# Gate tile of the dense experts in two buffers, v in three, and gate columns from two rounded matmuls per token

## The chip, the cores and the metric

The kernel runs on one core of one Trainium2 chip. The metric is the device time of one execution in microseconds (us). The core has five engines that run beside each other, each through its own list of instructions in a fixed order: PE (TensorE, matmuls; PEld is its loading of weights), DVE (VectorE), ACT (ScalarE), POOL (GpSimd) and SP (SyncE, which here only issues DMA transfers). An instruction starts when its turn has come on its engine and the results and buffers that it needs are there.

## The reference

One layer of a hybrid encoder on 1024 tokens of width 1024: an attention branch and a convolution branch, gated and merged, and then a layer of 128 x 128 single-neuron experts (PEER), of which each token uses 16 for each of 8 heads. The change lies in this last layer.

```python
def peer_ffn(hn, w_query, sub_keys, expert_u, expert_v):
    ...
        q = (xc @ w_query).reshape(c, PEER_HEADS, 2, PEER_HALF_DIM)
        sc = jnp.einsum('chpd,hpnd->chpn', q, sub_keys).astype(jnp.float32)
        s1, i1 = lax.top_k(sc[:, :, 0], PEER_TOPK)
        s2, i2 = lax.top_k(sc[:, :, 1], PEER_TOPK)
        cand = (s1[..., :, None] + s2[..., None, :]).reshape(c, PEER_HEADS, PEER_TOPK * PEER_TOPK)
        cidx = (i1[..., :, None] * PEER_N_KEYS + i2[..., None, :]).reshape(c, PEER_HEADS, PEER_TOPK * PEER_TOPK)
        top, pos = lax.top_k(cand, PEER_TOPK)
        eidx = jnp.take_along_axis(cidx, pos, axis=-1)
        g = jax.nn.softmax(top, axis=-1)
        u = expert_u[eidx]
        a = jax.nn.gelu(jnp.einsum('chkd,cd->chk', u, xc), approximate=False)
        vv = expert_v[eidx]
        return jnp.einsum('chk,chkd->cd', (g.astype(a.dtype) * a), vv)
```

## The kernel before

**Precision.** The large matmuls keep float32 precision by splitting each operand into a high part in the rounded 32-bit format (F32R) and a low part, the rest, in the same format. ACT writes the high part, DVE subtracts it to get the low one, and three products (high by high, high by low, low by high) are added in PSUM.

**Two groups of tokens.** Group B is five tiles of 128 tokens (`NB`), group A is three (`NA`). B goes through projection, attention, convolution, output and scores first, then A does. The scores of A are the last matmuls ahead of the expert layer.

**The two ways through the expert layer.** Group B is computed densely: all 128 rows of 128 experts are multiplied by all 640 tokens, and a gate matrix `w_d` in DRAM, zero wherever a token did not choose an expert, picks what counts. Group A gathers: for each token, POOL issues indirect DMAs that fetch the rows u and v of the chosen experts (`fetch`, L739, 384 transfers of 1 MB into `UVT` = 4 buffers), DVE forms the dot product with the token (L746) and, after two small ACT instructions (L748, L749), adds v times the result to `acc` (L755). The gather and the dense loop share DVE and the DMA engines.

**Selection.** `select_gen` finds the 16 best of each head on DVE with one multiply on POOL in each of its pieces (L639). A tile of tokens is selected in two halves, each of four heads. The five tiles of B feed the gate matrix, the three tiles of A the gather.

**The gate matrix.** `weights_gen` works in 160 steps of four tokens (`WQ`), 32 for each tile of B. In a step DVE compares the chosen row and column numbers with a row of counters, which gives two one-hot blocks `ms` (L714). POOL multiplies the first by the gate weights to `o1` (L718, the tile is shown as o), ACT copies the second to `o2` (L720), PE forms one 128 x 128 product for each of the four tokens (`pw`, L695), ACT copies them to `wbuf` (L696), and every eighth step the buffer goes to `w_d` (L726). The trace shows two records for each such float32 product, 1280 in all. `weights_gen`, the selection and the gather are generators: the phases that run beside them call `tick`, which lets them emit a step after so many estimated microseconds. The framework's scheduler then orders the emitted instructions on each engine by its own estimate of times.

**The dense loop.** For expert row i, `expert_in` loads u (`raw`, L913), splits it, forms `z` by 48 matmuls of 320 columns (L905), applies Gelu (L929) and multiplies by the gate tile `wt` (L930), which is loaded for four rows at once (`WB`, 1.28 MB, L920). The product is split to `ph`, `phl`. `expert_v` loads and splits v (`vh`, `vhl`). `expert_out` handles a pair of rows (`BLK`): 60 matmuls of 512 columns; two of the five token tiles stay in PSUM (`held`), three go through two PSUM buffers (`pout`) and are added to `hacc` by DVE (L957). All loads of u, v and wt are issued by SP in one queue.

```python
            wts[b] = dn.tile([P, GB // WT, WB, WT], F32, name="wt", tag="wt", bufs=1)
            SP.dma_start(out=wts[b], in_=w_d[:, :, i:i + WB, :].rearrange("c p i t -> p c i t"))
```

## Time and profile before

| what | value |
|---|---|
| time, median of 3 runs | 3235.85 us (3223.81 to 3254.53) |
| time of the profiled execution | 3236.47 us |
| its span, first to last instruction | 3234.7 us |
| busy share of the span | PE 93%, DVE 82%, ACT 40%, POOL 30% |
| mean granted TensorE clock | 0.973 of full speed |
| first and last Gelu of the dense loop | 1323.0 and 3153.1 us |
| last addition to hacc | 3181.1 us |

Times in the rows are counted from the start of the span. The shares are averages over the whole program; the stages are the projection and attention of B (to about 724 us), attention, convolution and output of A with most of the gate matrix beside them (to 1204), the scores of A (to 1312), the dense loop with the gather beside it (to 3181), and what is left of the gather (to the end).

### The profile page before, as it was taken

The numbers are of one execution on the slowest core, as the hardware profiler recorded it, in microseconds if no ns is written. First come the engines' busy times: TensorE is split into PE (matmuls) and PEld (weight loads), VectorE is DVE, ScalarE is ACT, GpSimd is POOL, SyncE is SP. The second block draws the span as 40 slices with busy tenths as digits, with TensorE's granted clock in tenths as the row PEclk, the third lists the DMA queues.
The fourth block names the chain that finished last, engine by engine and source line by source line (L and its number), as shares of the span: only waits on it lengthen the run. The fifth ranks groups of instructions, "written<-read, shape, count | busy, mean of one in ns | idle before, by whom it ended". The sixth has DMA issues, their size and how long they took to land.

```text
span 3234.7 us, 46047 instructions
## 1 busy us (share of the span) xinstructions
PE 3017.4 (93%) x17551; PEld 2768.1 (86%) x17551; DVE 2647.0 (82%) x4665; ACT 1298.3 (40%) x2344; POOL 954.6 (30%) x716
## 2 busy tenths in 40 slices
PE   7999999898999889799999999999999999999992
PEld 6799988798888779798989989889888999998891
DVE  4442565478999996798999999999999999998898
ACT  3322464335567757433333333333333333333332
POOL 2310000045444444232223323322333323233333
PEclk9999999999999989899999999999999999999996
DMA  5451232555444374787888888878789899988997
GB/s 177 146 177 66 82 111 92 211 164 202 146 177 182 148 269 161 265 297 274 304 291 293 308 286 315 323 275 316 268 301 339 325 348 338 339 329 317 327 331 288
DMA packets 237550, 801.12 MB, mean 248 GB/s; under 512 B 18832, under 2 KB 123280, under 8 KB 174096
## 3 DMA queue, kind: packets, MB, share of 16 engines
q0 software_dynamic: 64704, 442.53, 37.4%
q1 hardware_dynamic: 152592, 305.30, 27.2%
q10 hardware_dynamic: 20032, 50.34, 4.1%
q8 instruction: 138, 2.26, 0.3%
q14 instruction: 84, 0.69, 0.1%
HBM read 714.74 MB, written 83.36 MB: 247 GB/s over the span
## 4 chain that ended last, share of the span: by engine, by line
PE 36%; DVE 20%; issue 18%; DMA 15%; POOL 7%; ACT 3%; SPq 0%; POOLq 0%; ACTq 0%; DVEq 0%
DMA wt<-w_d 7%; PE z L905 7%; POOL uvt L739 6%; PE pg L228 4%; DMA uvt<-in_uv,idx 4%; PE pq L228 4%; PE pout L905 4%; DVE acc L755 3%; PE ph L228 3%; DVE uvt L746 3%; PE held L905 2%; PE py L228 2%; PE pw L695 2%; DVE hacc L957 2%; PE pv L228 1%
## 5 line engine op out<-in xcount | busy, mean ns | idle before, releaser
L739 POOL DMA_INDIRECT uvt<-in_uv,idx x384 | 552.6, 1439 | 1297.0 <-DVE acc L755 852.8
L905 PE MATMUL z<-actTh,uh 128*128 128x320 f32 x2048 | 636.7, 311 | 2.1 <-ACT pr L929 1.1
L905 PE MATMUL z<-actTh,uhl 128*128 128x320 f32 x2048 | 637.6, 311 | 0.0
L905 PE MATMUL z<-actTl,uh 128*128 128x320 f32 x2048 | 636.1, 311 | 0.0
L746 DVE SCALAR_TENSOR_TENSOR uvt<-uvt,hng 128x1024 f32<-128x1024 f32 x384 | 472.7, 1231 | 48.6 <-DMA uvt<-in_uv,idx 42.9
L755 DVE SCALAR_TENSOR_TENSOR acc<-uvt,wt,acc 128x1024 f32<-128x1024 f32 x381 | 486.4, 1277 | 6.1 <-ACT wt L749 4.8
L905 PEld LDWEIGHTS z<-actTh,uh 128*128 128x128 f32 x2048 | 387.1, 189 | 12.2 <-ACT pr L929 2.1
L905 PEld LDWEIGHTS z<-actTl,uh 128*128 128x128 f32 x2048 | 387.4, 189 | 8.8
L905 PEld LDWEIGHTS z<-actTh,uhl 128*128 128x128 f32 x2048 | 387.9, 189 | 4.0
L905 PE MATMUL pout<-vh,ph 128*128 128x512 f32 x768 | 306.5, 399 | 47.0 <-DVE hacc L957 30.2
L748 ACT ACTIVATE wt<-zt 128x1 f32<-128x1 f32 x384 | 77.5, 202 | 668.4 <-DVE uvt L746 667.5
L905 PE MATMUL pout<-vhl,ph 128*128 128x512 f32 x768 | 302.7, 394 | 0.0
L905 PE MATMUL pout<-vh,phl 128*128 128x512 f32 x768 | 301.9, 393 | 0.6 <-DVE phl L898 0.6
L718 POOL TENSOR_TENSOR o<-ms,wtr 128x512 f32<-128x512 bf16 x160 | 204.7, 1322 | 256.5 <-PE pw L695 127.3
L957 DVE TENSOR_TENSOR hacc<-pout,hacc 128x512 f32<-128x512 f32 x384 | 260.5, 681 | 2.8 <-PE pout L905 2.8
L185 DVE TENSOR_TENSOR wl<-wr,wh 128x2048 fp32r<-128x2048 f32 x66 | 157.2, 2382 | 118.8 <-ACT wh L184 114.7
L896 ACT CAST ph<-pr 128x640 fp32r<-128x640 f32 x128 | 93.3, 729 | 394.2 <-DVE pr L930 394.2
L905 PEld LDWEIGHTS pout<-vh,ph 128*128 128x128 f32 x768 | 145.7, 190 | 78.7 <-DVE hacc L957 39.5
L695 PE MATMUL pw<-o,o 128*128 128x128 f32 x1280 | 172.3, 288 | 39.8 <-POOL o L718 20.2
L184 ACT CAST wh<-wr 128x2048 fp32r<-128x2048 f32 x74 | 141.1, 1909 | 168.8 <-DMA wr<-in_wq 41.5
L695 PEld LDWEIGHTS pw<-o,o 128*128 128x128 f32 x1280 | 164.3, 201 | 47.7 <-POOL o L718 26.9
L905 PE MATMUL held<-vh,ph 128*128 128x512 f32 x512 | 200.6, 392 | 0.7 <-ACT ph L896 0.7
(290 smaller groups left out, 6760.4 us busy)
## 6 DMA issues: line engine op xcount, KB each, us to landing
raw<-in_uT SPq DMA_DIRECT2D x128, 512.0 KB, 6.5
raw<-in_uv SPq DMA_DIRECT2D x128, 512.0 KB, 8.0
w_d<-wbuf ACTq DMA_DIRECT2D x20, 2048.0 KB, 7.0
wt<-w_d SPq DMA_DIRECT2D x32, 1280.0 KB, 16.0
wr<-in_wcols SPq DMA_DIRECT2D x28, 1024.0 KB, 5.1
wr<-in_wq SPq DMA_DIRECT2D x24, 1024.0 KB, 5.2
xt<-in_x SPq DMA_DIRECT2D x16, 512.0 KB, 4.0
q_d<-qt POOLq DMA_DIRECT2D x32, 256.0 KB, 3.5
```

Source lines behind the costliest of these rows:

```text
L184: A.copy(out=op[0][sl], in_=src)
L185: lo.tensor_sub(op[1][sl], src, op[0][sl].bitcast(F32))
L228: PE.matmul(pd, lhsT=l[a], rhs=r[b], start=i == 0 and j == 0, stop=i == n - 1 and j == len(c) - 1)
L695: PE.matmul(pw[:, u, :], lhsT=o2[:, t + u, :], rhs=o1[:, t + u, :], start=True, stop=True)
L718: PL.tensor_tensor(out=o1.rearrange("p t i -> p i t"), in0=ms[:, 0], in1=w[:, ts].unsqueeze(1).broadcast_to(sh), op=ALU.mult)
L739: PL.indirect_dma_start(out=t[:], out_offset=None, in_=uv, in_offset=bass.IndirectOffsetOnAxis(ap=sels[c][1][:, k:k + 1], axis=0))
L746: V.scalar_tensor_tensor(u, u, 1.0, st[c], op0=ALU.mult, op1=ALU.mult, accum_out=zt)
L748: A.activation(wt, zt, AF.Gelu)
L755: V.scalar_tensor_tensor(st["acc"], v, wt, st["acc"], op0=ALU.mult, op1=ALU.add)
L896: A.copy(out=hi, in_=t)
L905: PE.matmul(ps, lhsT=lhs[k][a], rhs=rhs[k][b], start=first and k == 0 and j == 0, stop=last and k == n - 1 and j == 2)
L957: V.tensor_add(hacc[:, t - NR, ds], ps, hacc[:, t - NR, ds])
```

## The change

The gate tile `wt` gets two buffers where it had one. To make room, the tiles vh and vhl get three buffers where they had four, `weights_gen` uses one buffer for its weights and its counters where it had two, and the output phase of group A has one row buffer fewer. In `weights_gen` the two one-hot blocks are written in the rounded format F32R, and the gate weight is split into a high part (ACT) and a low part (DVE): POOL now makes two multiplies in a step, one for each part, and PE forms two F32R products for each token, added in PSUM, where it formed one product in float32.

```diff
-VHB = 4
+VHB = 3
...
-    def repeated_iota(pl, dst, tag="iota"):
+    def repeated_iota(pl, dst, tag="iota", bufs=2):
         n = dst.shape[1]
-        row = pl.tile([P, n], F32, name="iota", tag=tag, bufs=2)
+        row = pl.tile([P, n], F32, name="iota", tag=tag, bufs=bufs)
...
-            wk = pool("mixw", nt + MIXW, stack=st)
+            wk = pool("mixw", nt + MIXW - (tt0 > 0), stack=st)
...
-        repeated_iota(wf, iota_t, "wtr")
+        repeated_iota(wf, iota_t, "wtr", 1)
...
                 for u in range(4):
-                    PE.matmul(pw[:, u, :], lhsT=o2[:, t + u, :], rhs=o1[:, t + u, :], start=True, stop=True)
+                    for j in range(2):
+                        PE.matmul(pw[:, u, :], lhsT=o2[:, t + u, :], rhs=o1[:, j, t + u, :],
+                                  start=j == 0, stop=j == 1)
...
-            w = wf.tile([P, P], F32, name="wtr", tag="wtr", bufs=2)
-            A.copy(out=w, in_=pt[:, 2, :])
+            w = wf.tile([P, 2, P], F32R, name="wtr", tag="wtr", bufs=1)
+            A.copy(out=w[:, 0, :], in_=pt[:, 2, :])
+            V.tensor_sub(w[:, 1, :], pt[:, 2, :], w[:, 0, :].bitcast(F32))
...
-                    o1 = wf.tile([P, WQ, NK], F32, name="o1", tag="o1")
-                    o2 = wf.tile([P, WQ, NK], F32, name="o2", tag="o2")
-                    PL.tensor_tensor(out=o1.rearrange("p t i -> p i t"), in0=ms[:, 0],
-                                     in1=w[:, ts].unsqueeze(1).broadcast_to(sh), op=ALU.mult)
+                    o1 = wf.tile([P, 2, WQ, NK], F32R, name="o1", tag="o1")
+                    o2 = wf.tile([P, WQ, NK], F32R, name="o2", tag="o2")
+                    for j in range(2):
+                        PL.tensor_tensor(out=o1[:, j].rearrange("p t i -> p i t"), in0=ms[:, 0],
+                                         in1=w[:, j, ts].bitcast(F32).unsqueeze(1).broadcast_to(sh), op=ALU.mult)
                     A.copy(out=o2.rearrange("p t i -> p i t"), in_=ms[:, 1])
...
-            wts[b] = dn.tile([P, GB // WT, WB, WT], F32, name="wt", tag="wt", bufs=1)
+            wts[b] = dn.tile([P, GB // WT, WB, WT], F32, name="wt", tag="wt", bufs=2)
```

The scheduler orders all instructions anew, and three places change. In the lists below a name's number only tells one tile from another; in the changed kernel the lines lie four further down in the dense loop and the gather (L917 is L913, L924 is L920, L909 is L905, L759 is L755, L961 is L957), and L696 is L695.

The first place is SP's queue in the middle of the dense loop, before. A load of u is raw from in_uT, a load of v raw from in_uv; the first of the four rows that use wt_17305 has its u in raw_17307.

```order
L920 DMA wt_16734<-w_d_76 128x20x128
L913 DMA raw_17154<-in_uv 128x1024
L913 DMA raw_17160<-in_uT 128x1024
L913 DMA raw_17299<-in_uv 128x1024
L913 DMA raw_17307<-in_uT 128x1024
L913 DMA raw_17441<-in_uv 128x1024
L913 DMA raw_17447<-in_uT 128x1024
L913 DMA raw_17575<-in_uv 128x1024
L913 DMA raw_17581<-in_uT 128x1024
L920 DMA wt_17305<-w_d_76 128x20x128
```

The same queue after; wt_16974 belongs to the row whose u is raw_16976.

```order
L924 DMA wt_16974<-w_d_76 128x20x128
L917 DMA raw_16694<-in_uv 128x1024
L917 DMA raw_16700<-in_uT 128x1024
L917 DMA raw_16834<-in_uv 128x1024
L603 DMA sc_18056<-sc_d_68 128x1024
L917 DMA raw_16840<-in_uT 128x1024
L917 DMA raw_16968<-in_uv 128x1024
L917 DMA raw_16976<-in_uT 128x1024
L917 DMA raw_17111<-in_uv 128x1024
L917 DMA raw_17117<-in_uT 128x1024
L924 DMA wt_17539<-w_d_76 128x20x128
```

Before, the load of a gate tile stands five raw loads behind the u of its own first row; after, it stands six raw loads ahead of it.

The second place is PE between the last scores of group A (pcs) and the first matmul of the dense loop (z), before. One row of pw is one step of `weights_gen`.

```order
L695 MATMUL pw<-o_10523,o_10524 128x128 x4
L564 MATMUL pcs<-sk,qp 128x128 x3
L695 MATMUL pw<-o_10535,o_10536 128x128 x4
L564 MATMUL pcs<-sk,qp 128x128 x3
L695 MATMUL pw<-o_10547,o_10548 128x128 x4
L695 MATMUL pw<-o_10559,o_10560 128x128 x4
L905 MATMUL z<-actTh,uh 128x320
```

The same place after, the beginning; 27 such rows of pw x8 follow each other there, the last of which is `pw<-o_11355,o_11356`, and then comes z.

```order
L564 MATMUL pcs<-sk,qp 128x128 x3
L696 MATMUL pw<-o_10557,o_10558 128x128 x8
L564 MATMUL pcs<-sk,qp 128x128 x3
L696 MATMUL pw<-o_10579,o_10580 128x128 x8
L696 MATMUL pw<-o_10635,o_10636 128x128 x8
L696 MATMUL pw<-o_10652,o_10653 128x128 x8
L696 MATMUL pw<-o_10681,o_10682 128x128 x8
L696 MATMUL pw<-o_10688,o_10689 128x128 x8
L696 MATMUL pw<-o_10733,o_10734 128x128 x8
```

Before, two steps stand between the last score and the first z, after, 27 do. Counted on the same lists, the scores of A begin with 128 steps done before and 106 after, and on DVE the first half of A's selection ends at the last step before and at step 134 after; two more halves, which stood in the dense loop, stand between that step and step 160.

The third place is the end of DVE's list, before; the last addition to hacc stands further up, and 13 additions to acc follow it.

```order
L755 SCALAR_TENSOR_TENSOR acc<-uvt,wt,acc 128x1024
L746 SCALAR_TENSOR_TENSOR uvt,zt<-uvt,hng 128x1024
L755 SCALAR_TENSOR_TENSOR acc<-uvt,wt,acc 128x1024
L768 TENSOR_TENSOR uvt<-uvt,acc 128x1024
L167 TENSOR_SCALAR m_o<-ss_o 128x1
L176 SCALAR_TENSOR_TENSOR uvt<-uvt,r_o 128x1024
```

The same end after.

```order
L759 SCALAR_TENSOR_TENSOR acc<-uvt,wt,acc 128x1024
L961 TENSOR_TENSOR hacc<-pout,hacc 128x512 x2
L167 TENSOR_SCALAR m_h<-ss_h 128x1
L772 TENSOR_TENSOR uvt<-uvt,acc 128x1024
L176 SCALAR_TENSOR_TENSOR raw<-raw,r_h,fin_d 128x1024
L961 TENSOR_TENSOR hacc<-pout,hacc 128x512
```

After, the last addition to acc stands ahead of the last four additions to hacc, and none follows them.

## Rows read from the trace of the kernel before

**Rows 1.** Busy time by stage: us, then PE, PEld, DVE, ACT, POOL, PEclk, DMA share, GB/s

```profile
724.00:1204.00 480.00, 423.20 (x2687) 400.91 (x2688) 451.71 (x1200) 321.16 (x471) 218.32 (x162) 0.95 0.50 184
1204.00:1312.00 108.00, 105.68 (x722) 104.60 (x721) 75.41 (x172) 71.77 (x103) 45.98 (x35) 1.00 0.47 173
1346.00:2560.00 1214.00, 1183.41 (x6536) 1071.93 (x6537) 1129.03 (x1822) 404.46 (x818) 369.83 (x243) 0.99 0.83 299
2560.00:3153.00 593.00, 588.38 (x3276) 535.68 (x3275) 546.49 (x695) 203.32 (x436) 182.01 (x132) 1.00 0.91 332
3181.00:3234.70 53.70, 0.00 (x0) 0.00 (x0) 38.00 (x48) 10.29 (x34) 17.15 (x15) 0.50 0.73 275
```

**Rows 2.** Gelu, whole program, then 2673.4 to 2896.5: ns min/median/max, first to last start

```profile
L929 ACT ACTIVATE pr<-z x128: 682/696/708, 1323.0 to 3153.1; 128x640 f32<-128x640 f32 x128
...
L929 ACT ACTIVATE pr<-z x17: 682/696/701, 2673.5 to 2896.4; 128x640 f32<-128x640 f32 x17
```

**Rows 3.** The gate tile wt: its user, its wait (us, times), its loads

```profile
L930 DVE TENSOR_TENSOR pr<-pr,wt x128: 802/815/2543, 1346.0 to 3155.7; 128x640 f32<-128x640 f32 x128
...
  DMA wt<-w_d: 91.5, 24
...
DMA to landing us min/median/max: 9.1/16.0/22.7
```

**Rows 4.** Waits of PE, 1321 to the end: total us, times, longest

```profile
PE pout L905 <- DVE hacc L957: 30.2, 23, 5.3
```

**Rows 5.** The page's groups: busy us, mean ns, then idle before, releaser

```profile
L746 DVE SCALAR_TENSOR_TENSOR uvt<-uvt,hng 128x1024 f32<-128x1024 f32 x384 | 472.7, 1231 | 48.6 <-DMA uvt<-in_uv,idx 42.9
...
L718 POOL TENSOR_TENSOR o<-ms,wtr 128x512 f32<-128x512 bf16 x160 | 204.7, 1322 | 256.5 <-PE pw L695 127.3
...
L695 PE MATMUL pw<-o,o 128*128 128x128 f32 x1280 | 172.3, 288 | 39.8 <-POOL o L718 20.2
```

**Rows 6.** The chain of waits from the scores into the dense loop: start, us, what

```profile
1302.66 1.79 PE pw L695 x16
...
1315.83 10.15 DMA w_d<-wbuf
1325.98 0.02 issue
1326.00 20.01 DMA wt<-w_d
```

**Rows 7.** Timeline of POOL, then of DVE, at the last steps: start, us

```profile
1308.89 2.62 POOL L718 TENSOR_TENSOR o<-ms,wtr 128x512 f32<-128x512 bf16 x2
1312.26 1.19 POOL L718 TENSOR_TENSOR o<-ms,wtr 128x512 f32<-128x512 bf16 x1 [0.74 <-DVE idx L679]
...
1308.87 0.68 DVE L714 TENSOR_TENSOR ms<-ib,iota_t 128x1024 bf16<-128x1024 bf16 x1
...
1311.44 0.67 DVE L714 TENSOR_TENSOR ms<-ib,iota_t 128x1024 bf16<-128x1024 bf16 x1
1312.04 0.21 DVE L679 SCALAR_TENSOR_TENSOR idx<-e,e 128x64 int32<-128x64 f32 x1
```

**Rows 8.** The one-hots by line, 724 to 1204: busy us, mean ns, idle before

```profile
L714 DVE TENSOR_TENSOR ms<-ib,iota_t 128x1024 bf16<-128x1024 bf16 x128 | 103.9, 822 | 6.5 <-ACT o L720 4.9 <-POOL o L718 1.4
```

**Rows 9.** F32R matmuls of 128 columns: timeline, start and us, then all by line

```profile
33.91 0.79 PE L191 MATMUL pt<-ident_r,kst 128*128 128x128 f32 x8
...
L191 PE MATMUL pt<-ident_r,kst x64: 222/244/252, 33.9 to 178.8; 128*128 128x128 f32 x64
```

**Rows 10.** First half of A's selection begins (DVE); POOL's part of selections

```profile
1276.89 1.26 DVE L588 MAX8 sv<-sc 128x8 f32<-128x128 f32 x6 [2.25 <-DMA sc<-sc_d]
...
L639 POOL TENSOR_TENSOR sc<-sc,sf x32: 1929/1942/6253, 683.1 to 2349.6; 128x1024 bf16<-128x1024 bf16 x32
```

**Rows 11.** The end: additions to acc after 3181 us, last output, by line and timeline

```profile
L755 DVE SCALAR_TENSOR_TENSOR acc<-uvt,wt,acc x14: 1269/1284/1320, 3179.9 to 3225.0; 128x1024 f32<-128x1024 f32 x14
...
3225.04 1.28 DVE L755 SCALAR_TENSOR_TENSOR acc<-uvt,wt,acc 128x1024 f32<-128x1024 f32 x1 [0.60 <-ACT wt L749]
...
3230.95 0.34 SPq L770 DMA_DIRECT2D out<-uvt  x1
```

## The prediction

> **What bounds the kernel now.** I read the stages first, since the shares of the whole span hide them. The stage table [rows 1] shows three bounds. From 724 to 1204 us DVE is busy 452 of 480 us and PE 423: two engines are nearly full, and the gate matrix is made in their gaps. In the scores of A PE is busy 105.7 of 108 us. In the dense loop PE is busy 97 to 99% and DVE 92 to 93%. After 3181 PE has no work at all: there DVE finishes the gather alone, for 53.7 us.
>
> The second view is the spacing of the Gelus [rows 2], one for each expert row. From 3153.1 back to 1323.0 there are 127 intervals; measured from the first gate multiply at 1346.0 to the last at 3155.7 [rows 3], they take 1809.7 us, 14.25 each. In an undisturbed stretch 16 intervals take 222.9 us, 13.93 each. So the loop can win at most 127 x 0.32 = 41 us unless PE itself gets less to do, and it does not.
>
> Third, the wait that the second buffer is to remove. DVE stood 91.5 us before the gate multiply for a wt load, 24 times; a load lands in 16.0 us [rows 3]. But DVE is not the bound there. What PE saw of DVE's lateness is 30.2 us of waits for hacc, 23 of them [rows 4]. The 91.5 us are therefore not the prize; some 30, and at most 41, are.
>
> Fourth, the way into the loop. The chain of waits runs from the last pw over the write of wbuf (10.2 us) and the load of wt (20.0 us) to the first gate multiply [rows 6]: the last step of the gate matrix, and nothing else, lets the loop start. The last one-hot ends at 1312.1 [rows 7], the first multiply comes at 1346.0.
>
> **724 to 1204.** The instruction lists say that 106 steps are done at its end in place of 128. That takes 22 x 0.82 = 18 us from DVE [rows 8]. PE had about 1280 / 160 = 8 records in a step, in 0.89 us (16 in 1.79) [rows 6]. Now it has 8 F32R matmuls; the nearest row is a run of eight of 128 columns in 0.79 us, of which one alone takes 0.244, so a further one costs (0.79 - 0.244) / 7 = 0.078 us, and eight in a stream 0.62 [rows 9]. PE has 128 x 0.89 - 106 x 0.62 = 48 us less. Neither is gained in full, as the other inputs of the stage (weight loads, attention's softmax) keep their order. Against it, POOL's part grows from 128 to 212 multiplies of 1.32 us [rows 5], and a one-hot beside it takes 0.82 us on average here [rows 8], 0.68 where it runs free [rows 7]. If that excess of 0.14 grows with POOL's work, it is 106 x 0.14 = 15 us back. I take -8, with ends of -20 (all DVE relief) and +20 (the excess twice over and a few later weight loads). The row buffer less in the output phase can only delay a load: 0 to 5 us, taken as 0, since no wait for it stands in the chain. Beside the 480 us the new low-part subtraction, 128 x 128 five times, is below 2 us; the tile of weights in one buffer holds up one step at each new tile of tokens, also about that.
>
> **The scores of A.** PE is the bound. 32 steps of 0.89 us become about 25 of 0.62: 28.5 - 15.5 = 13 us less [rows 1, 6, 9]. The stage goes from 108 to 95, and its end no longer opens the dense loop, because 27 steps are left.
>
> **The steps left over.** The first half of A's selection ends on DVE at step 134. Before, it came 108 us after the scores began (1312.0); I take 101, being between the full 13 us and none, as it needs the scores of a whole tile and then DVE. From there 26 steps remain, and two more halves of the selection stand between them on DVE. What is one step worth when POOL sets the pace? Two multiplies back to back with a one-hot at their side took 2.62 us, one alone 1.19 [rows 7]. Low end: 2 x 1.19 = 2.38; high end: plus a whole one-hot, 3.06. I take 2.62, the row that has just this pair: 26 x 2.62 = 68. The two halves put four POOL multiplies of 1.94 us into the same list [rows 10]: 8. DVE has as much there: the half that is seen whole ran from 1276.9 to 1312.3, 35.4 us with ten one-hots (6.7) and one weight subtraction (2.3) in it, so it needs about 26, and 2 x 26 + 26 x 0.68 = 70 us. Two engines with 70 to 76 us each that wait on each other do not overlap fully: I add 6, making 82, with ends of 70 and 95. PE, ACT and SP do nothing else meanwhile: PE's next instruction is z, behind the last pw. So nothing covers these 82 us; queued behind them is the whole dense loop.
>
> From the last multiply to the first gate multiply I keep 32.6 us (1346.0 - 1313.4 [rows 3, 7]), as the write and the first load are the same. The first gate multiply comes at 1204 - 8 + 101 + 82 + 32.6 = 1411.6: **66 us later**, ends +40 and +95.
>
> **The dense loop.** The load of wt goes from five raw loads behind its first user to six ahead of it. The longest load took 22.7 us [rows 3], so the wait should go. Two halves of selection, 52 us of DVE, have left the loop too. With both, intervals go from 14.25 to about 14.02, not to 13.93, since DVE stays above 90% and the gather stays: 128 x 0.22 = **-28 us**; ends -41 (13.93 throughout) and -5. v in three buffers cannot gain by itself. The second v of a pair can only be cast when the last matmul of the pair before is done, half a pair interval (7 us) before its use; cast and subtraction are below 2 us, so I price it at 0, with +5 as the upper end if DVE is in the middle of a pair of long gather instructions.
>
> **The end.** Before, the last additions to acc run to 3226.3, and the output is issued at 3230.95 [rows 11], 75 us after the last gate multiply. In the lists after, the last addition to acc stands before the last additions to hacc, so the gather has caught up: A's selection is ready earlier relative to the loop. Then 28 us (3153 to 3181) of remaining products and some 11 of normalising and writing follow the last Gelu, about 42 in place of 82: **-40**; ends -43 and -25, if the chip's gather falls behind the scheduler's.
>
> **Sum.** +66 - 28 - 40 = -2 on the profiled execution's 3236.5, whose span is 3234.7 and which lies within 1 us of the median: **3234 us**. A change of 1% (32 us) is about what can be told from none.
>
> **Rivals.** *POOL and DVE shut each other out.* Every one-hot reads two tiles from SBUF, and so does every POOL multiply. If the two never overlap, a step costs 2 x 1.19 + 0.68 = 3.06: 26 x 0.44 = 11 us more in the exposed steps; and up to 1204 the added 106 multiplies of 1.2 us fall on a DVE with 28 us of slack [rows 1]. At a third of them in DVE's way, 42 - 15 (the excess already counted) = 27 more. Sum 3234 + 38 = 3272, slower. For it: the one-hots' 0.82 against 0.68 [rows 7, 8]. Against it: 0.14 of excess is far from a whole 1.19. It decides once the weights' lateness passes the 68 us that the loop and the end give back, by 32.
>
> The Trainium skill, "SBUF — State Buffer", section "Who interferes with whom", speaks for this rival: a DVE instruction with two SBUF inputs contends with a GpSimd instruction that reads SBUF, and the shared pair is an exclusive lock. Rows 7 fit it: 2 x 1.19 and one overlap of 0.24, though not a full 0.68 on either side. By the rule taken strictly the time would be that 3272; by the row, 3234.
>
> *POOL is quicker, and DVE and PE free.* With 2.38 us in a step (62 + 8, no loss by waiting), -20 up to 1204 and the full 13.93 in the loop, the weights come 42 us late, and the sum is 42 - 41 - 40 = -39: 3197. For it: PE's and DVE's real relief. Against: DVE at 93 and 92% of the loop [rows 1] has little slack left when two long instructions meet, and the waits for gathered rows [rows 5] stay.
>
> *The wait moves.* Without wt the loop may wait for raw or the gather: the DMA engines are at 0.91 late [rows 1], and DVE already stood 42.9 us for gathered rows [rows 5]. Then the loop gives 0, and the sum is +26: 3262.
>
> *The change does not do what it says.* If a matmul in the new format costs what one alone takes, 0.22 [rows 9], a step costs PE 8 x 0.22 = 1.8: scores +29 us against my sum, and 75 us more PE up to 1204 where 57 are free, some 35 of it paid: about 3298.
>
> **How the numbers follow.** The forecast has 0.50 (3210 to 3260 with its own ends), shut-out 0.15, quicker 0.17, moved wait 0.13, costly matmuls 0.05. The range of 3190 to 3285 reaches over the quick case and the shut-out and leaves out the costly matmuls and the far ends. Faster than 3203 holds the quick case and a little of the forecast, less the part of the quick case above it: 0.22. Slower than 3268 holds the shut-out, the matmuls and a third of the moved wait, with the forecast's upper tail: 0.27. Same: 0.51.
>
> **What would show it.** After: PE idle for most of some 80 us between the last pcs and the first z, with POOL near full there; POOL's o x320; pw matmuls in F32R with a pitch near 0.08; the first gate multiply near 1412; no wait for wt; Gelu intervals near 14.0; the last acc before the last hacc. The prediction is wrong if the first multiply comes before 1386 or after 1440, if the intervals stay at 14.2, or if additions to acc still run alone at the end.

## The result and the profile after

The changed kernel takes 3269.63 us (median of 11 runs, 3262.25 to 3277.49) against 3236.97 us for the kernel before on the same chips: ratio 1.0096, 95% interval 1.0074 to 1.0117. It is slower by about 33 us. The range held it, the forecast of no change did not: the kernel moved, by about the 1% that the prediction called the least that can be told from none. The profiled execution has a span of 3272.7 us.

Three numbers place the difference: when the first gate multiply starts, how long the loop takes from the first to the last gate multiply, and what follows. Predicted and measured, against 1346.0, 1809.7 and 79.0 us before [rows 3]:

| term | predicted | measured in the profiles |
|---|---|---|
| scores of A begin (before: 1203.8) | -8 | 1248.4: +45 |
| scores of A, first to last matmul (before: 108.6) | -13 | 108.9: 0 |
| last score to first gate multiply (before: 34) | +87 | 108: +74 |
| first gate multiply | +66 | 1465.2: +119 |
| loop | -28 | 1772.9: -37 |
| from the last gate multiply to the end | -40 | 34.6: -44 |
| sum | -2 | +38 |

The stage table of the kernel after, with the columns of [rows 1]; the stages are the attention and output of A, its scores, the steps left over, the loop, and the end.

```profile
724.00:1248.00 524.00, 433.77 (x2508) 404.84 (x2509) 486.19 (x1200) 291.04 (x429) 334.84 (x252) 0.87 0.44 160
1248.00:1357.00 109.00, 106.21 (x704) 105.39 (x702) 75.37 (x162) 66.77 (x97) 76.75 (x56) 0.97 0.46 164
1357.00:1449.00 92.00, 55.72 (x219) 49.15 (x219) 86.78 (x259) 47.25 (x61) 70.37 (x56) 0.50 0.30 113
1465.00:3238.00 1773.00, 1768.32 (x9866) 1611.30 (x9866) 1666.80 (x2339) 616.13 (x1281) 545.18 (x387) 1.00 0.90 326
3238.00:3272.70 34.70, 15.39 (x60) 10.29 (x58) 27.94 (x40) 10.05 (x20) 6.44 (x7) 0.81 0.52 192
```

The first row is the surprise. DVE is as full as before (486 of 524 us, 452 of 480 then), but has 34 us more to do although 18 one-hots fewer stand in the stretch (110; 128 then). Pieces of the selection have moved up in their place: both stretches count 1200 instructions, and with each form at the shortest duration that any of these runs shows the list is only 5 us shorter than before. In the third row DVE is busy 87 of 92 us, POOL 70, and PE, with little to do, runs at a granted clock of 0.50, the lower of its two levels. In the fourth PE is busy 1768 of 1773 us.

The gate tile, whole program, in the columns of [rows 3]: its user, and what DVE and others stood idle for.

```profile
L934 DVE TENSOR_TENSOR pr<-pr,wt x128: 790/818/852, 1465.2 to 3238.1; 128x640 f32<-128x640 f32 x128
...
  ACT pr L933: 34.7, 33
  DMA wt<-w_d: 2.3, 1
```

The wait for wt fell from 91.5 us, 24 times, to 2.3 us, once. The gate multiply now waits for the Gelu (34.7 us, 33 times), so DVE is early where it was late. PE's wait for hacc, 30.2 us before [rows 4], in the same view of the kernel after:

```profile
PE pout L909 <- DVE hacc L961: 3.2, 5, 1.0
```

The costliest groups of the page, for the two operations that the change doubles or replaces [rows 5]; then the one-hots by line, 724 to 1248 [rows 8]; then PE's timeline in the scores of A, where two steps stand in a row.

```profile
L722 POOL TENSOR_TENSOR o<-ms,wtr 128x512 fp32r<-128x512 bf16 x320 | 406.8, 1345 | 188.0 <-DVE ms L717 106.7
...
L696 PE MATMUL pw<-o,o 128*128 128x128 f32 x1280 | 218.2, 314 | 89.9 <-POOL o L722 52.6
```

```profile
L717 DVE TENSOR_TENSOR ms<-ib,iota_t 128x1024 bf16<-128x1024 bf16 x110 | 104.9, 958 | 2.2 <-POOL o L722 1.4 <-ACT ib L707 0.7
```

```profile
1255.92 1.90 PE L696 MATMUL pw<-o,o 128*128 128x128 f32 x16
1257.66 0.39 PE L228 MATMUL pq<-hnTl,wh 128*128 128x384 f32 x1
```

POOL has its 320 multiplies, a little dearer than before (1345 ns, 1322). A one-hot takes 0.96 us where it took 0.82. Sixteen records of pw fill PE from 1255.92 to 1257.66: 0.109 us each, 0.87 a step. Before, two steps that stand in the same place take 0.107 us each, 0.86 a step:

```profile
1302.49 1.95 PE L695 MATMUL pw<-o,o 128*128 128x128 f32 x16
1304.20 0.42 PE L228 MATMUL pq<-hnTh,wh 128*128 128x384 f32 x1
```

The rounded pair costs PE what the one float32 product did.

How POOL and DVE meet is best seen beside each other. DVE's timeline, two stretches of the first stage of the kernel after, and then POOL's in the same stretches:

```profile
724.03 1.93 DVE L634 SCALAR_TENSOR_TENSOR pf<-ti,pi 128x64 bf16<-128x64 uint32 x1
725.88 4.54 DVE L649 TENSOR_TENSOR e<-tv,zz 128x64 f32<-128x64 f32 x1
...
1176.42 0.18 DVE L632 TENSOR_SCALAR pi<-ti 128x64 uint32<-128x64 uint32 x1
1176.53 0.18 DVE L633 TENSOR_SCALAR pj<-ti 128x64 uint32<-128x64 uint32 x1
1176.63 1.97 DVE L649 TENSOR_TENSOR e<-tv,zz 128x64 f32<-128x64 f32 x1
1178.52 0.55 DVE L822 TENSOR_TENSOR gb<-gb,ga 128x384 f32<-128x384 f32 x1
```

```profile
723.95 1.93 POOL L639 TENSOR_TENSOR sc<-sc,sf 128x1024 bf16<-128x1024 bf16 x1 [9.52 <-issue]
725.84 4.50 POOL L185 TENSOR_TENSOR wl<-wr,wh 128x2048 fp32r<-128x2048 f32 x1
...
1176.58 1.93 POOL L639 TENSOR_TENSOR sc<-sc,sf 128x1024 bf16<-128x1024 bf16 x1 [1.00 <-DVE sc L637]
```

The e of L649 takes 0.21 us at its shortest. Beside a POOL subtraction of 4.50 us it takes 4.54, beside a POOL multiply of 1.93 it takes 1.97: it ends when POOL's instruction ends. The two TENSOR_SCALARs ahead of it take their 0.18, but they start before POOL does. One input is no protection: beside four multiplies in a row (POOL in the last line) the same kind of instruction takes 1.10.

```profile
1102.82 1.10 DVE L628 TENSOR_SCALAR pi<-ti 128x64 uint32<-128x64 uint32 x1
1103.79 1.10 DVE L629 TENSOR_SCALAR pj<-ti 128x64 uint32<-128x64 uint32 x1
...
1101.78 4.06 POOL L722 TENSOR_TENSOR o<-ms,wtr 128x512 fp32r<-128x512 bf16 x4 [1.92 <-PE pw L696]
```

Three groups of DVE up to the scores, first before, then after. The inputs of e and of y (a sum of the convolution) lie in SBUF, but gb has one input, py, in PSUM:

```profile
L649 DVE TENSOR_TENSOR e<-tv,zz 128x64 f32<-128x64 f32 x7 | 3.2, 461 | 0.0
L487 DVE SCALAR_TENSOR_TENSOR y<-z,cw_t,y 128x384 f32<-128x384 f32 x4 | 2.4, 610 | 0.0
L520 DVE SCALAR_TENSOR_TENSOR gb<-gb,py 128x384 f32<-128x384 f32 x8 | 4.3, 537 | 0.0
...
L649 DVE TENSOR_TENSOR e<-tv,zz 128x64 f32<-128x64 f32 x8 | 12.1, 1518 | 0.0
L487 DVE SCALAR_TENSOR_TENSOR y<-z,cw_t,y 128x384 f32<-128x384 f32 x4 | 5.2, 1307 | 0.0
L520 DVE SCALAR_TENSOR_TENSOR gb<-gb,py 128x384 f32<-128x384 f32 x8 | 4.3, 542 | 0.0
```

This holds for the whole list. Added up over the stretch, the durations above the shortest of each form are 57 us before and 97 after for instructions with two inputs in SBUF, 0.6 us both times for those with one of two inputs in PSUM, and 21 and 22 us for those with one input. The growth is all in the first kind.

### The profile page after: what moved, and what is told of

It reads as the page before. It is cut to its first block, busy times and chain, and to the rows that moved or that the text cites. A ratio compares the mean times of both kernels' runs of the same rounds, so it can differ in the third digit from the quotient of the medians.

```text
span 3272.7 us, 46086 instructions
## 1 busy us (share of the span) xinstructions
PE 3070.5 (94%) x17551; PEld 2816.9 (86%) x17551; DVE 2710.0 (83%) x4670; ACT 1303.1 (40%) x2340; POOL 1136.6 (35%) x876
## 4 chain that ended last, share of the span: by engine, by line
PE 47%; issue 18%; DVE 17%; POOL 8%; DMA 7%; ACT 2%; SPq 0%; POOLq 0%; DVEq 0%; ACTq 0%
PE z L909 13%; PE pout L909 7%; POOL uvt L743 7%; PE held L909 5%; PE pq L228 4%; PE pg L228 4%; DMA uvt<-in_uv,idx 2%; DVE ms L717 2%; PE ph L228 2%; PE py L228 2%; DVE acc L759 1%; PE pk L228 1%; DVE e L640 1%; PE po L228 1%; PE pv L228 1%
## 5 line engine op out<-in xcount | busy, mean ns | idle before, releaser
L743 POOL DMA_INDIRECT uvt<-in_uv,idx x384 | 536.7, 1398 | 1236.5 <-DVE acc L759 1056.5
L909 PE MATMUL z<-actTh,uh 128*128 128x320 f32 x2048 | 638.5, 312 | 5.4 <-ACT pr L933 4.7
L909 PE MATMUL z<-actTh,uhl 128*128 128x320 f32 x2048 | 638.6, 312 | 0.5 <-DVE uhl L902 0.5
L909 PE MATMUL z<-actTl,uh 128*128 128x320 f32 x2048 | 637.4, 311 | 0.0
L750 DVE SCALAR_TENSOR_TENSOR uvt<-uvt,hng 128x1024 f32<-128x1024 f32 x384 | 469.2, 1223 | 30.1 <-DMA uvt<-in_uv,idx 26.0
L759 DVE SCALAR_TENSOR_TENSOR acc<-uvt,wt,acc 128x1024 f32<-128x1024 f32 x381 | 486.1, 1276 | 1.1 <-ACT wt L753 1.1
L722 POOL TENSOR_TENSOR o<-ms,wtr 128x512 fp32r<-128x512 bf16 x320 | 406.8, 1345 | 188.0 <-DVE ms L717 106.7
L909 PEld LDWEIGHTS z<-actTh,uh 128*128 128x128 f32 x2048 | 388.2, 190 | 17.8 <-ACT pr L933 6.9
L909 PEld LDWEIGHTS z<-actTl,uh 128*128 128x128 f32 x2048 | 388.4, 190 | 9.3
L909 PEld LDWEIGHTS z<-actTh,uhl 128*128 128x128 f32 x2048 | 388.8, 190 | 6.2 <-DVE uhl L902 1.0
L909 PE MATMUL pout<-vh,ph 128*128 128x512 f32 x768 | 300.2, 392 | 3.2 <-DVE hacc L961 3.2
L696 PE MATMUL pw<-o,o 128*128 128x128 f32 x1280 | 218.2, 314 | 89.9 <-POOL o L722 52.6
L909 PE MATMUL pout<-vhl,ph 128*128 128x512 f32 x768 | 300.2, 391 | 0.0
L909 PE MATMUL pout<-vh,phl 128*128 128x512 f32 x768 | 299.9, 391 | 0.0
L696 PEld LDWEIGHTS pw<-o,o 128*128 128x128 f32 x1280 | 202.0, 229 | 109.4 <-POOL o L722 79.6
L961 DVE TENSOR_TENSOR hacc<-pout,hacc 128x512 f32<-128x512 f32 x384 | 259.9, 683 | 26.0 <-PE pout L909 25.5
L933 ACT ACTIVATE pr<-z 128x640 f32<-128x640 f32 x128 | 90.3, 705 | 324.8 <-PE z L909 318.0
L724 ACT CAST o<-ms 128x512 fp32r<-128x512 bf16 x160 | 177.5, 1118 | 88.9 <-DVE ms L717 79.1
L909 PE MATMUL held<-vhl,ph 128*128 128x512 f32 x512 | 198.7, 390 | 0.0
```

Source lines behind the costliest of these rows:

```text
L696: PE.matmul(pw[:, u, :], lhsT=o2[:, t + u, :], rhs=o1[:, j, t + u, :], start=j == 0, stop=j == 1)
L722: PL.tensor_tensor(out=o1[:, j].rearrange("p t i -> p i t"), in0=ms[:, 0], in1=w[:, j, ts].bitcast(F32).unsqueeze(1).broadcast_to(sh), op= ...
L724: A.copy(out=o2.rearrange("p t i -> p i t"), in_=ms[:, 1])
L743: PL.indirect_dma_start(out=t[:], out_offset=None, in_=uv, in_offset=bass.IndirectOffsetOnAxis(ap=sels[c][1][:, k:k + 1], axis=0))
L750: V.scalar_tensor_tensor(u, u, 1.0, st[c], op0=ALU.mult, op1=ALU.mult, accum_out=zt)
L759: V.scalar_tensor_tensor(st["acc"], v, wt, st["acc"], op0=ALU.mult, op1=ALU.add)
```

## The experiments

All twelve kernels in one table, from their profiled executions; each ratio is to the kernel before on the same chip.

| kernel | ratio (95% interval) | scores of A begin | first gate multiply | loop | end |
|---|---|---|---|---|---|
| before | 1 | 1204 | 1346.0 | 1809.7 | 79.0 |
| changed | 1.0096 (1.0074, 1.0117) | 1248 | 1465.2 | 1772.9 | 34.6 |
| buf_alone | 0.9864 (0.9823, 0.9904) | 1202 | 1344.1 | 1785.8 | 62.9 |
| gate_alone | 1.0225 (1.0180, 1.0269) | 1250 | 1468.6 | 1802.5 | 37.8 |
| one_mult | 0.9897 (0.9858, 0.9935) | 1221 | 1360.3 | 1784.9 | 53.8 |
| write_only | 0.9932 (0.9905, 0.9960) | 1209 | 1387.9 | 1779.6 | 46.0 |
| write_twice | 0.9998 (0.9982, 1.0013) | 1212 | 1424.0 | 1778.3 | 35.4 |
| two_mult_f32 | 1.0103 (1.0069, 1.0137) | 1253 | 1449.8 | 1776.4 | 45.6 |
| one_matmul | 0.9826 (0.9794, 0.9857) | 1206 | 1344.2 | 1784.5 | 49.9 |
| v3_alone | 0.9913 (0.9888, 0.9938) | 1202 | 1334.2 | 1810.0 | 61.9 |
| act_low | 1.0213 (1.0188, 1.0239) | 1265 | 1485.0 | 1778.0 | 36.9 |
| swap | 0.9902 (0.9874, 0.9929) | 1215 | 1396.0 | 1773.6 | 40.1 |

### The two halves of the change

The kernel before with the buffers alone, and the changed kernel with the buffers put back:

```diff
 (buf_alone, against before)
-VHB = 4
+VHB = 3
-            wts[b] = dn.tile([P, GB // WT, WB, WT], F32, name="wt", tag="wt", bufs=1)
+            wts[b] = dn.tile([P, GB // WT, WB, WT], F32, name="wt", tag="wt", bufs=2)
 (gate_alone, against the changed kernel)
-VHB = 3
+VHB = 4
-            wts[b] = dn.tile([P, GB // WT, WB, WT], F32, name="wt", tag="wt", bufs=2)
+            wts[b] = dn.tile([P, GB // WT, WB, WT], F32, name="wt", tag="wt", bufs=1)
```

> The kernel before with the gate tile in two buffers and v in three, gate columns as before. Theory 1 (the buffer gives the gain of the dense loop, the second POOL multiply costs what it lost): first gate multiply stays near 1346 us, no wait for wt, the loop from first to last gate multiply falls from 1810 to about 1775, additions to acc behind the last one to hacc fall from 13 to about 9; time 3175 to 3200. Theory 2 (the loop got shorter because two halves of the selection had left it, the buffer only moves the wait to other transfers): loop stays above 1795, time 3215 or more.

> The changed kernel with the gate tile back in one buffer and v in four. Theory 1: first gate multiply as late as in the changed kernel (1465 within 10), the loop keeps most of its waits for wt and is 1790 to 1805, little or no gather left at the end; time 3290 to 3320. Theory 2: the loop is as short as in the changed kernel (1773) without the second buffer; time near 3270.

The gate tile in buf_alone, and then in gate_alone, in the columns of [rows 3]:

```profile
L930 DVE TENSOR_TENSOR pr<-pr,wt x128: 802/820/2559, 1344.1 to 3129.9; 128x640 f32<-128x640 f32 x128
...
  DMA wt<-w_d: 10.2, 1
```

```profile
L934 DVE TENSOR_TENSOR pr<-pr,wt x128: 804/818/2006, 1468.6 to 3271.1; 128x640 f32<-128x640 f32 x128
...
  DMA wt<-w_d: 93.0, 28
```

Theory 1 holds for both, though the loop of buf_alone, expected near 1775, takes 1786. The buffers gain 1.4%, the gate columns lose 2.3%, and 0.9864 x 1.0225 = 1.0086 lies inside the change's interval. The loop falls by 24 us in buf_alone (1809.7 to 1785.8), by 7 in gate_alone, where two halves of the selection have left it (to 1802.5), and by 37 with both. In the end part most of the gain comes with the late start (37.8 in gate_alone): the gather is further on when the loop is over.

### Which part of the gate columns costs

one_mult makes the second product from a tile of zeros, one_matmul drops it, and two_mult_f32 puts the second multiply alone into buf_alone. All have two gate buffers and three for v.

```diff
 (one_mult, against the changed kernel)
+        zero = wf.tile([P, NK], F32R, name="zero", tag="zero", bufs=1)
+        V.tensor_scalar(zero, iota_t[:, :, 0], 0.0, None, op0=ALU.mult)
-                        PE.matmul(pw[:, u, :], lhsT=o2[:, t + u, :], rhs=o1[:, j, t + u, :],
+                        PE.matmul(pw[:, u, :], lhsT=o2[:, t + u, :], rhs=o1[:, 0, t + u, :] if j == 0 else zero,
-                    o1 = wf.tile([P, 2, WQ, NK], F32R, name="o1", tag="o1")
+                    o1 = wf.tile([P, 1, WQ, NK], F32R, name="o1", tag="o1")
-                    for j in range(2):
+                    for j in range(1):
                         PL.tensor_tensor(out=o1[:, j].rearrange("p t i -> p i t"), in0=ms[:, 0],
 (one_matmul, against one_mult)
-                    for j in range(2):
-                        PE.matmul(pw[:, u, :], lhsT=o2[:, t + u, :], rhs=o1[:, 0, t + u, :] if j == 0 else zero,
-                                  start=j == 0, stop=j == 1)
+                    for j in range(1):
+                        PE.matmul(pw[:, u, :], lhsT=o2[:, t + u, :], rhs=o1[:, 0, t + u, :],
+                                  start=True, stop=True)
 (two_mult_f32, against buf_alone, with the changed kernel's economies of space)
+                    o3 = wf.tile([P, WQ, NK], F32, name="o3", tag="o3", bufs=1)
+                    PL.tensor_tensor(out=o3.rearrange("p t i -> p i t"), in0=ms[:, 0],
+                                     in1=w[:, ts].unsqueeze(1).broadcast_to(sh), op=ALU.mult)
```

> The changed kernel without the second POOL multiply: the low part of the gate weight is left out, and the second F32R matmul of each token multiplies a tile of zeros instead, so that PE does the same number of matmuls. Theory 1: with one multiply in a step the lateness goes: scores of A begin near 1204 (1195 to 1215), first gate multiply 1325 to 1355, time as in buf_alone within 15. Theory 3 (the lateness comes from the format's matmuls, 0.87 us a step as before and waits that let the clock fall, and from the new order): scores begin after 1230 and the first gate multiply after 1400, time above 3230.

> one_mult without its second matmul: one multiply and four F32R matmuls in a step (the low part of the gate weight is left out). A matmul of 128 columns with its own weight load takes 0.11 us of PE in both kernels, so PE has 0.44 us less in a step than in one_mult. If PE's share in the steps matters ahead of the loop: scores of A take 92 to 96 us (105 in one_mult, 104 before), and the time is 8 to 25 us below one_mult (3206). If DVE alone sets the stretch: the scores still take 100 or more, or the loop starts no earlier, and the time is within 6 of one_mult.

> The kernel before with the gate tile in two buffers and v in three, as in buf_alone, and a second POOL multiply in each step whose result nobody reads; the gate columns stay single float32 products. It takes the changed kernel's economies of space (weights and counters in one buffer, one row buffer less in the output phase of A). Theory 1 (the second multiply is what costs): as late as the changed kernel, scores of A after 1235 and first gate multiply 1420 to 1470, time 3240 to 3275. Theory 3 (the rounded format or its two matmuls cost): near buf_alone, first gate multiply below 1380, time 3190 to 3215.

With one multiply the first gate multiply comes back from 1465 to 1360, with a second one and float32 products it goes from 1344 (buf_alone) to 1450. So it is the multiply, not the format. one_mult missed its own numbers by a little: scores began at 1221, first gate multiply at 1360. The last step of the gate matrix was done earlier there (last pw at 1315), but ACT then stood at a gather instruction ahead of the first rounding of u, and PE with it, 21.07 us by PE's own timeline (first line; the second is ACT's, whose wt is a small tile of the gather):

```profile
1349.05 0.63 PE L911 MATMUL z<-actTh,uh 128*128 128x320 f32 x1 [21.07 <-ACT uh L902]
...
1340.31 0.20 ACT L754 ACTIVATE wt<-zt 128x1 f32<-128x1 f32 x1 [9.97 <-DVE uvt L752]
```

In one_matmul, with four matmuls of PE less in a step, the scores of A fall from 107 us (1221 to 1328) to 93 (1206 to 1299), as 0.44 us times some 27 steps would have it, and the time to 0.9826. Fewer matmuls would have shortened the scores; the change does not have fewer.

### POOL's time or POOL's reading

write_only and write_twice put instructions that read nothing in the place of the second multiply. write_twice keeps the lists of PE and DVE almost as they are in the changed kernel.

```diff
                     for j in range(2):
-                        PL.tensor_tensor(out=o1[:, j].rearrange("p t i -> p i t"), in0=ms[:, 0],
-                                         in1=w[:, j, ts].bitcast(F32).unsqueeze(1).broadcast_to(sh), op=ALU.mult)
+                    PL.tensor_tensor(out=o1[:, 0].rearrange("p t i -> p i t"), in0=ms[:, 0],
+                                     in1=w[:, 0, ts].bitcast(F32).unsqueeze(1).broadcast_to(sh), op=ALU.mult)
 (write_only)
+                    PL.iota(o1[:, 1].rearrange("p t i -> p (t i)"), pattern=[[0, WQ * NK]], base=0, channel_multiplier=0, allow_small_or_imprecise_dtypes=True)
 (write_twice)
+                    for _ in range(2):
+                        PL.memset(o1[:, 1].bitcast(F32), 0.0)
```

> The changed kernel with the second POOL multiply replaced by a POOL iota that writes zeros to the same tile and reads nothing from SBUF (the low part of the gate weight is left out). Theory 1a (DVE instructions are stretched because POOL reads SBUF beside them): DVE's one-hots beside it take as long as in the kernel before (0.82 us mean up to the scores) or less, scores begin by 1215, time within 25 of one_mult. Theory 1b (any second POOL instruction stretches DVE or delays the steps): one-hots at 0.9 us or more, scores begin after 1225, time above 3220.

> The changed kernel with the second POOL multiply replaced by two POOL memsets of the same tile, which write zeros and read nothing (the low part of the gate weight is left out). The instruction lists of PE and DVE stay almost those of the changed kernel: 132 steps done at the last score (133 there), halves of the selection at steps 135, 151, 160 (134, 150, 160). Theory 1a (POOL's reading of SBUF stretches DVE): the one-hots' mean up to the scores is below 0.87 us (0.96 in the changed kernel, 0.82 before), scores of A begin by 1220 (1248), first gate multiply by 1430 (1465), time 3215 to 3240. Theory 1b (POOL's time in a step and the new order suffice): scores begin after 1235, first gate multiply after 1450, time above 3255.

In write_only the scores begin at 1209, and the time stays within 10 us of one_mult, as theory 1a has it; the one-hots, at 0.838, miss its 0.82.

write_twice by line, 724 to 1212, and its first stage in the columns of [rows 1]:

```profile
L721 POOL TENSOR_TENSOR o<-ms,wtr 128x512 fp32r<-128x512 bf16 x108 | 152.2, 1410 | 122.7 <-PE pw L696 53.3 <-issue 27.6 <-DVE ms L717 26.6
...
L724 POOL MEMSET o<- 128x512 f32 x214 | 112.1, 545 | 4.7 <-PE pw L696 3.6
L717 DVE TENSOR_TENSOR ms<-ib,iota_t 128x1024 bf16<-128x1024 bf16 x110 | 94.8, 874 | 11.3 <-POOL o L724 4.8 <-ACT o L725 4.3 <-ACT ib L707 1.4
L649 DVE TENSOR_TENSOR e<-tv,zz 128x64 f32<-128x64 f32 x8 | 6.1, 757 | 0.0
L487 DVE SCALAR_TENSOR_TENSOR y<-z,cw_t,y 128x384 f32<-128x384 f32 x4 | 3.0, 738 | 0.0
```

```profile
724.00:1212.00 488.00, 426.21 (x2512) 399.66 (x2512) 446.75 (x1202) 290.28 (x430) 310.74 (x358) 0.89 0.47 170
```

POOL's part of a step is 1.41 + 2 x 0.545 = 2.50 us, not far from 2 x 1.353 = 2.7 in the changed kernel, whose multiplies take 1.353 on average up to its scores. DVE runs nearly the same list (1202 instructions, 1200 there) in 447 us instead of 486, and the scores begin at 1211.5 instead of 1248.4. The durations above the shortest, for two inputs in SBUF, are back at 59 us, from 97. So about 37 of the 45 us ahead of the scores come from DVE instructions that stand beside a reading POOL instruction; what the 0.2 us less of POOL in a step does to this was not separated. PE's clock does not explain it: the granted clock of this stretch is 0.89 here, 0.87 in the changed kernel and 0.95 before. The one-hots, at 0.874, and the time, at 3244, miss the limits of theory 1a by 4 ns and 4 us; the scores and the first gate multiply (1424) keep them. The steps left over take 88 us from the last score to the first z and 91 in the changed kernel: there POOL's and DVE's lists set the time, and reading adds 3 us.

Reading is not the larger part of the lateness. From buf_alone to the changed kernel the first gate multiply moves by 121 us (1344 to 1465), and write_twice, at 1424, has 80 of them though its second POOL instruction reads nothing. They are POOL's longer turn in a step and the order that comes with it, which leaves 28 steps behind the last score there, 27 in the changed kernel, and none in one_mult.

This is also what the Trainium skill states in "SBUF — State Buffer", section "Who interferes with whom": a DVE instruction with two SBUF inputs contends with a GpSimd instruction that reads SBUF, not with one that only writes it. These runs agree: e and y, above, take 0.76 and 0.74 us, against 1.52 and 1.31 in the changed kernel.

A DVE instruction with one input can be held up by a POOL instruction that only writes, too. In write_twice a CAST that takes 0.21 us at its shortest takes 1.35 and ends with the last of three memsets, and the durations of one-input instructions above their shortest grow from 22 us in the changed kernel to 43 (these records overlap each other, and DVE's busy time falls all the same).

```profile
879.15 1.35 DVE L611 CAST sf<-si 128x128 f32<-128x128 uint32 x1
...
878.90 1.52 POOL L724 MEMSET o<- 128x512 f32 x3
```

### Moving the multiply elsewhere

```diff
 (act_low, against the changed kernel)
-                    for j in range(2):
-                        PL.tensor_tensor(out=o1[:, j].rearrange("p t i -> p i t"), in0=ms[:, 0],
-                                         in1=w[:, j, ts].bitcast(F32).unsqueeze(1).broadcast_to(sh), op=ALU.mult)
+                    PL.tensor_tensor(out=o1[:, 0].rearrange("p t i -> p i t"), in0=ms[:, 0],
+                                     in1=w[:, 0, ts].bitcast(F32).unsqueeze(1).broadcast_to(sh), op=ALU.mult)
+                    for t in range(WQ):
+                        A.activation(o1[:, 1, t, :], ms[:, 0, :, t], AF.Copy,
+                                     scale=w[:, 1, b * WT + q + t:b * WT + q + t + 1].bitcast(F32))
 (swap, against buf_alone)
-                    PL.tensor_tensor(out=o1.rearrange("p t i -> p i t"), in0=ms[:, 0],
-                                     in1=w[:, ts].unsqueeze(1).broadcast_to(sh), op=ALU.mult)
-                    A.copy(out=o2.rearrange("p t i -> p i t"), in_=ms[:, 1])
+                    for t in range(WQ):
+                        A.activation(o1[:, t, :], ms[:, 0, :, t], AF.Copy, scale=w[:, b * WT + q + t:b * WT + q + t + 1])
+                    PL.tensor_copy(out=o2.rearrange("p t i -> p i t"), in_=ms[:, 1])
```

> The changed kernel with the second multiply of a step (the low part) made by four ACT instructions of 128 elements, each with the weight as its scale, in place of the POOL multiply; nothing is left out. The lists of PE and DVE stay almost those of the changed kernel (132 steps at the last score). Theory 1a (POOL's second read beside DVE is what stretches the front): one-hots up to the scores near 0.82 to 0.85 us, scores of A begin by 1220, first gate multiply 1395 to 1430, time 3205 to 3240. Theory 1b (two multiplies of any engine and the later order): scores after 1235, first gate multiply after 1445, time above 3255.

> buf_alone with the two engines' work exchanged: ACT makes the weighted one-hot in four instructions of 128 elements with the weight as scale, POOL copies the other one-hot; nothing is left out, float32 products as before. If POOL's multiply, with its two inputs in SBUF, is what stretches DVE (65 us of 724 to 1204 over the shortest durations), a copy with one input stretches it less: stretch below 45 us, scores of A begin by 1190, and the time falls 5 to 20 us below buf_alone (3194) if the steps left over (20 after the last score in the list, 2 in buf_alone) do not eat it. If a copy shuts DVE out as a multiply does: stretch stays at 60 or more and the time is 3200 to 3230.

ACT, DVE and PE by line in act_low, 724 to 1265, and then POOL in swap, 724 to 1215:

```profile
L724 ACT ACTIVATE o<-ms,wtr 128x128 fp32r<-128x128 bf16 x432 | 141.3, 404 | 24.6 <-DVE ms L717 21.9 <-PE pw L696 2.6
L726 ACT CAST o<-ms 128x512 fp32r<-128x512 bf16 x108 | 118.4, 1102 | 8.9 <-DVE ms L717 8.9
L717 DVE TENSOR_TENSOR ms<-ib,iota_t 128x1024 bf16<-128x1024 bf16 x110 | 88.3, 808 | 25.2 <-ACT o L726 16.4 <-ACT ib L707 5.7 <-ACT o L724 2.9
L696 PE MATMUL pw<-o,o 128*128 128x128 f32 x848 | 127.0, 302 | 44.1 <-ACT o L726 31.4 <-POOL o L721 9.4 <-ACT at L449 3.2
```

```profile
L720 POOL CAST o<-ms 128x512 f32<-128x512 bf16 x114 | 152.1, 1365 | 215.0 <-PE pw L695 100.9 <-DVE ms L714 63.6 <-DVE rz L396 18.6
```

Neither move gained anything. In act_low DVE is relieved as theory 1a has it (one-hots 0.81 us, 457 us busy up to the scores, 486 in the changed kernel), but the times are those of theory 1b (scores at 1265, first gate multiply at 1485, 3306 us), so this run does not tell the two apart as write_twice does: an ACT instruction of 128 elements takes 0.40 us, four of them and the other copy 2.7 us a step, and ACT, busy 410 us of 541, now makes the one-hots and PE wait. That ACT's turn is the new bound there is read from these waits, not tested. In swap the copy costs POOL 1.365 us, no less than the multiply, and nothing is won.

### v in three buffers

```diff
-VHB = 4
+VHB = 3
```

> The kernel before with v in three buffers and nothing else changed. Prediction's term: 0 to +5 us, time 3237 to 3247. Rival (the third buffer less delays the loop by more than that, and the gate tile's gain was larger than it looks): loop from first to last gate multiply above 1820 us, time 3255 or more.

```profile
L930 DVE TENSOR_TENSOR pr<-pr,wt x128: 790/820/830, 1334.2 to 3144.2; 128x640 f32<-128x640 f32 x128
...
  DMA wt<-w_d: 59.2, 21
```

Neither theory: the kernel is 0.9% faster. The loop did not change (1810.0 us). The first gate tile landed in 7.7 us after its issue at 1326.5, where it took 20.0 before [rows 6]; fewer other transfers stood beside it (up to 1334 us the DMA engines moved 226 GB/s, 373 before). The end part is 17 us shorter, with 371 of the gather's 384 dot products begun at the last Gelu instead of 365. Both probably follow from the new order of the instructions; why the scheduler's order came out denser with less space was not tested. In buf_alone the end part is 16 us shorter as well, but the first gate multiply is not early and the gain of 24 us lies in the loop. So the end's 16 us may be v's, the loop's 24 us need the second gate buffer, and the 0.9% is not simply a part of buf_alone's 1.4%; the gate buffer without v in three was not run.

## Why the prediction was wrong, step by step

**What bounds the kernel** was read rightly: the steps of the gate matrix open the loop, the gain in the loop is PE's 30 to 41 us and not DVE's 91.5 (37 measured), and the wait for wt goes.

**The loop and the end** were right, -28 and -40 predicted, -37 and -44 measured, the end just past its bound of -43.

**The steps left over** were right: from the last score to POOL's last multiply 88 us by the prediction's own numbers, 89 measured. Too dear were the 32.6 us from there to the first gate multiply, taken over from before; they were 19, as the first gate tile was there 9 us after its issue and not 20. So 121 us from the last score to the first gate multiply became 108.

**"724 to 1204 ... I take -8"** is the step that failed: the scores of A begin 45 us later, outside its ends of -20 and +20. The -8 is 15 us of stretching less 23 of relief, and both terms were mis-sized. DVE's stretching was counted for the one-hots alone; these measured just that, 110 x (0.958 - 0.822) = 15, but every other DVE instruction with two inputs in SBUF pays too, and DVE's whole list takes 39 us less when POOL's second instruction does not read (write_twice). And the relief was not there. DVE's 18 us were 5, since pieces of the selection moved up into the stretch, and PE's 48 were 7: pw kept it busy for 133 us up to the scores, 140 before. Even in write_twice the scores begin 8 us later than before.

**"The scores of A ... 13 us less"** failed for PE's part of that, with 0. The 0.078 us for a further matmul came from transposes [rows 9], another operation; a pw matmul with its weight load takes 0.11 us, in either format. The stage also holds 30 steps before and 27 after, not 32 and about 25, so that even at 0.62 us a step the gain would have been 10.

**"v in three buffers cannot gain by itself"** was wrong for the kernel before: alone it brought 0.9%, none of it in the loop, probably by another order of the instructions (v3_alone).

**Its own signs.** The wait for wt went, the gather ended ahead of the loop, and the first z waited for 27 steps. But the first gate multiply came at 1465, after its limit of 1440, the pitch of pw, the time from one matmul to the next, was 0.109 us and not near 0.08, and PE, meant to be idle for most of the steps left over, was busy 56 of 92 us at the lower clock.

**The rivals.** "POOL and DVE shut each other out" was the mechanism, and its 3272 us lies by the measured 3270; that it lies so near is partly luck. Up to 1204 it priced the shutting out at 42 us (27 on top of the 15 already counted), where write_twice shows about 37; "at a third of them in DVE's way" was a guess that no row supported and that happened to be near. In the steps left over it added 11 us, where write_twice shows 3. And it kept the forecast's relief: by its numbers the scores begin at 1223 and the first gate multiply comes at 1450 (measured: 1248 and 1465), and the loop and the end, 13 us better than forecast, make up for most of that. That the matmuls would not get cheaper was half of another rival, at 0.05; the other half, that they cost double, was wrong.

The best of these kernels that computes all of the reference is buf_alone, 0.9864; one_matmul, at 0.9826, leaves out the low part of the gate weight.

## What to carry to other kernels

Where POOL work is added beside a full DVE, price it on every DVE instruction of that stretch with both inputs in SBUF, not only on the one that shares its data, and look at DVE's casts and TENSOR_SCALARs too: the sign is a short instruction that ends when a POOL instruction ends. When steps are moved out of a stretch, count what moves in. Take the pace of a matmul from the same operation with its weight load, or from one whose weights come at the same rate. And split a change of two parts before keeping it: here 1.4% gained hid behind 2.3% lost, and v's buffer, priced at nothing, moved the time by 0.9% when changed alone.

## What the runs showed of the hardware

An e of 64 elements took 4.54 us beside a POOL subtraction of 4.50, and 0.21 at its shortest. DVE instructions with one of two inputs in PSUM were not stretched (gb, 0.54 us before and after). A TENSOR_SCALAR of 0.18 us took 1.10 beside POOL multiplies, and a CAST of 0.21 took 1.35 beside three memsets, which read nothing. Two F32R matmuls of 128 columns, each with its weight load, took 0.22 us of PE, like one float32 product, which the trace shows as two records. An ACT copy of 128 x 128 with a scale took 0.40 us, and one of 128 x 512 1.10; POOL's copy of 128 x 512 took as long (1.365) as its multiply, and a memset of that size 0.545.
